# The first weight transfers on ScalarE's queue, and the opening steps of a two-layer encoder in a new order

## The chip, the cores and the metric

The kernel runs on one core of one Trainium2 chip. The metric is the time of one execution on the device in microseconds (us), lower is better; a median of several executions is given. The engines are named as in the profile: PE (TensorE, matrix products), PEld (its weight loads), DVE (VectorE), ACT (ScalarE), POOL (GpSimd) and SP (SyncE, which here only issues transfers). A name with a q (SPq, ACTq) is an engine's instruction queue issuing a transfer.

## The reference, cut to what matters

A sequence of 256 rows of width 1024 passes two layers. Each layer is a half SwiGLU block, a mixer and another half SwiGLU block, each on the normalised rows. The change concerns the first 1.5% of the program: the first SwiGLU block, `swiglu(rmsnorm(x, norm_g[0, 0]), ...)`, and within it the first 512 of 2816 columns.

```python
def rmsnorm(x, g):
    x32 = x.astype(jnp.float32)
    y = x32 * lax.rsqrt(jnp.mean(x32 * x32, axis=-1, keepdims=True) + RMS_EPS)
    return (y * g.astype(jnp.float32)).astype(x.dtype)

def swiglu(h, w_gate, w_up, w_down):
    return (jax.nn.silu(h @ w_gate) * (h @ w_up)) @ w_down

for i in range(DEPTH):
    x = x + MACARON_WEIGHT * swiglu(rmsnorm(x, norm_g[i, 0]), ffn_w_gate[i, 0], ffn_w_up[i, 0], ffn_w_down[i, 0])
    ...
```

## The kernel before, in words

Every float32 product is made of three PE products of rounded halves: a matrix is split into a high part (one ACT copy with rounding, `split_hi`, line 246) and a low part (one subtraction on DVE or POOL, `split_lo`, line 250), and `mm3` (lines 265 to 267) adds high by high, high by low and low by high. The weights pass once: a transfer of 1 MB fills one of two `raw` buffers (four slabs of 128 rows by 512 columns), ACT and DVE split it into one of four `wh` and four `wl` buffers, PE reads these. A `raw` buffer is free for the next transfer when both splits of its four slabs have read it.

The program is a long PE stream; the first chunk of the first block is written out by hand as a list of steps, `START` (line 37), which `first` (line 480) issues one after the other under a manual schedule, so that PE, ACT, DVE and POOL each do their instructions in the order of the list. SP's transfers follow the list too. The steps are:

- `X t.k.n` loads n column blocks of row half t of x; `L u.c.n` loads n slabs of weight unit u from slab c; both on SP. `T` turns x on PE and scales it on DVE, `h` is its high part (ACT), `l` its low part on DVE, `G` its low part on POOL.
- `w u.c` is the high part of a weight slab (ACT), `a u.c` its low part on DVE, `y u.c` its low part on POOL.
- `M m.t.k` is one product of three matmuls: m is gate (0) or up (1), t the row half, k the block of 128 input columns. There are 32, 16 for gate and 16 for up. Block k = 0 must come first in its bank. Units 2 and 3 are the two halves of up, units 0 and 1 of gate; units 4 and 5 belong to the next chunk.
- `D` is a matmul on zeros that keeps PE busy, `g` turns the gains (`norm_g`), `B` and `R` make the row sums and their inverse roots (POOL), `A` applies silu and the product of the two halves.

Behind this list everything else is placed by the framework's scheduler, which estimates times itself and puts each engine's instructions in the order of its estimate; so the order of steps that the diff doesn't name can move as well. In what follows `decay` (line 616) loads a table into a `raw` buffer and takes its absolute value on DVE, `window` (line 621) makes four exponentials of it on ACT, `layer` (line 592) is a small network whose sine is on ACT, and `tr`/`down` (lines 453 and 464) turn the block's result, split it into `ph` and `pl` and multiply it into the `acc` banks. The tables `BUFFERS` (line 80) say which of the rotating buffers each allocation takes.

Of the kernel before, what the change touches and what calls it, by code (L numbers as in the profile page):

```python
# [12 lines left out]
F32 = mybir.dt.float32  # L13
F32R = mybir.dt.float32r
BF16 = mybir.dt.bfloat16
AF = mybir.ActivationFunctionType
# [5 lines left out]
P = 128  # L22
D = 1024
# [6 lines left out]
W = 512  # L30
# [4 lines left out]


START = (
# [7 lines left out]
)  # L45
MIX = (
# [32 lines left out]

BUFFERS = {  # L80
    "mm": (
        "0123012301231023013132103213021302132013201320132012301320132031203120321032103210321021231023102310",
        "2301230123102310321032013201230132013201230123013201321032102310230123102310231232013203103213013210",
        "132302301230132013021322103210320132013210321023102301230132012",
    ),
    "acc": (
        "01230123102301230130213030213021302130213021302012103120312",
# [3 lines left out]
        "010101010101010101010101011010101010101010101010101010101",  # L91
    ),
    "wh": (
        "0123012301230123013021302130213021302130231023102310231023102310231023102310231023102310231023102310",
        "2310231023102310231021302103210321032103210321032103210",
    ),
    "wl": (
        "0123012301230123013021302130213021302130231023102310231023102310231023102310231023102310231023102310",
        "2310231023102310231021032130213021302130213021302130213",
    ),  # L100
    "ph": (
        "012340124301243012432342013240312403124031240314203142031423014201320410214341203412034120341",
# [77 lines left out]
class Net:  # L180
# [139 lines left out]
    def load(self):  # L320
        nc, a, const = self.nc, self.a, self.const
        self.ident = const.tile([P, P], F32, name="ident")
        make_identity(nc, self.ident)
        self.wake = self.scr.tile([P, W], BF16, name="sq", bufs=1)
        nc.vector.memset(self.wake, 0.0)
        self.vr = self.h()[:48, :P]
        nc.sync.dma_start(out=self.vr, in_=a["norm_g"].rearrange("i j (k p) -> (i j k) p", p=P))
        self.x = [const.tile([P, D], F32, name=f"x{t}") for t in range(NT)]
        self.mhalf = const.tile([P, 1], F32, name="mhalf")
        nc.vector.memset(self.mhalf, -0.5)  # L330
        warm = const.tile([P, 1], F32, name="warm")
        nc.scalar.activation(warm, self.mhalf, AF.Silu)
        self.ones = const.tile([P, P], F32, name="ones")
        nc.vector.memset(self.ones, 1.0)
        self.g = const.tile([P, 48], F32, name="g")
        self.gain = lambda i, j: self.g[:, (3 * i + j) * KC:(3 * i + j + 1) * KC]

    def load_gain(self):
        ps = self.bank()
        self.nc.tensor.transpose(out=ps[:, :48], in_=self.vr, identity=self.ident[:48, :48])  # L340
        self.nc.vector.tensor_copy(out=self.g, in_=ps[:, :48])
# [41 lines left out]
    def ffn(self, r, xT, late, wg, wu, wd, finish, hooks=(), early=None, mid=None, pre=None, tail=False):  # L383
        nc, x = self.nc, self.x
# [95 lines left out]
        def first():  # L480

            st, raws, tiles = {}, {}, {}
# [3 lines left out]
                c = slice(k * P, (k + n) * P)  # L486
                nc.sync.dma_start(out=x[t][:, c], in_=self.a["x"][0, halves(t), c])

            def load_w(u, c, n):

                if u not in raws:
                    raws[u] = self.place(self.raw, "raw", U)
                    tiles[u] = self.place(self.wp, "wh", U, F32R), self.place(self.wp, "wl", U, F32R)
                nc.sync.dma_start(out=raws[u].rearrange("p (k c) -> p k c", k=4)[:, c:c + n],
                                  in_=self.rows((wg, wu, wg)[u // 2], u % 2 * 4 + c, n, u // 4 * W, W))

            def turn(t, k, n):
# [8 lines left out]
            def x_parts(t, k, n):  # L506
                return (xh[:, k:k + n, halves(t)], xl[:, k:k + n, halves(t)],
                        st["x", t, k][:, :n * P].rearrange("p (k c) -> p k c", k=n))
# [14 lines left out]
            def rstd(t):  # L523
                r[t], _ = self.rstd([st["s", t, half] for half in range(2)])

            do = {
                "X": load_x, "L": load_w, "D": self.spin, "g": self.load_gain, "T": turn,
                "h": lambda t, k, n: self.split_hi(*x_parts(t, k, n)),
                "l": lambda t, k, n: self.split_lo(*x_parts(t, k, n)),
                "G": lambda t, k, n: self.split_lo(*x_parts(t, k, n), True),  # L530
# [22 lines left out]
        for t in range(NT):  # L553
# [4 lines left out]
            for half in range(2):  # L558
# [3 lines left out]
                n = W // 2 if tail and t and half else W  # L562
# [176 lines left out]
    def mixer(self, hy, mx, cur, nxt, wg, pre, hold, dump=None):  # L739
# [207 lines left out]
        def late_turn():  # L947
            state["late"] = cur["late_turn"]()

        load(6)  # L950
        for c in range(4):
            piece_hi(6, c)
# [42 lines left out]
    def mla(self, ml, cur, nxt, wg, pre, hold, after, dump=None):  # L995
# [314 lines left out]
        def next_split(t, half):  # L1310
            hold[:] = nxt["split"](t, half, state["x", t, half])

        load(0)
        for c in range(4):
            piece_hi(0, c)
# [174 lines left out]
```

## Time and profile before

| | us |
|---|---|
| median of 3 executions | 963.69 |
| lowest, highest | 962.13, 964.54 |
| the profiled execution | 963.41 |
| span in the profile (first to last instruction) | 961.6 |
| PE busy in the span | 950.8 |

The profiled execution spends 1.8 us outside its span. Shares of the span by engine on the chain that ended last, starts and durations of instructions, and the time from issuing a transfer to its landing are used below. A PE row's duration is modelled and overlaps the next row; what a matmul costs is the distance between the starts of two rows, 0.227 us for 512 columns.

### The profile page before, as it was taken

The numbers are of one execution on the slowest core, as the hardware profiler recorded it, in microseconds if no ns is written. First come the engines' busy times: TensorE is split into PE (matmuls) and PEld (weight loads), VectorE is DVE, ScalarE is ACT, GpSimd is POOL, SyncE is SP. The second block draws the span as 40 slices with busy tenths as digits, with TensorE's granted clock in tenths as the row PEclk, the third lists the DMA queues.
The fourth block names the chain that finished last, engine by engine and source line by source line (L and its number), as shares of the span: only waits on it lengthen the run. The fifth ranks groups of instructions, "written<-read, shape, count | busy, mean of one in ns | idle before, by whom it ended". The sixth has DMA issues, their size and how long they took to land.

```text
span 961.6 us, 12376 instructions
## 1 busy us (share of the span) xinstructions
PE 950.8 (99%) x4792; PEld 802.0 (83%) x4792; DVE 592.1 (62%) x786; ACT 495.4 (52%) x780; POOL 179.2 (19%) x228
## 2 busy tenths in 40 slices
PE   9999999999999999999999999999999999999997
PEld 6878888889998888888888888888899888888885
DVE  5577777968876654545565454445787665444454
ACT  5565665447456444445454443334688664333442
POOL 1500441415755100000020000000266510000000
PEclk9999999999999999999999999999999999999999
DMA  7757665436233765455546555554142465556531
GB/s 262 244 178 219 199 235 185 158 100 187 89 132 132 240 215 201 175 175 178 194 139 226 205 182 207 177 210 153 58 135 89 150 222 188 205 178 208 184 132 44
DMA packets 80778, 168.09 MB, mean 175 GB/s; under 512 B 3820, under 2 KB 24181, under 8 KB 80336
## 3 DMA queue, kind: packets, MB, share of 16 engines
q1 hardware_dynamic: 79232, 164.79, 50.3%
q0 software_dynamic: 1200, 1.99, 0.7%
q8 instruction: 37, 0.61, 0.3%
q10 hardware_dynamic: 288, 0.52, 0.1%
q14 instruction: 21, 0.17, 0.1%
HBM read 165.72 MB, written 1.05 MB: 173 GB/s over the span
## 4 chain that ended last, share of the span: by engine, by line
PE 95%; DVE 2%; DMA 1%; issue 1%; ACT 1%; SPq 0%; POOLq 0%; POOL 0%; DVEq 0%; ACTq 0%
PE mm L266 18%; PE mm L265 18%; PE mm L267 18%; PE acc L265 10%; PE acc L267 10%; PE acc L266 10%; PE mm L270 4%; PE acc L789 2%; PE acc L790 1%; PE acc L788 1%; DMA raw<-ffn_w_up 1%; DVE wl L250 0%; PE mm L1272 0%; PE mm L1271 0%; PE mm L1273 0%
## 5 line engine op out<-in xcount | busy, mean ns | idle before, releaser
L250 DVE TENSOR_TENSOR wl<-raw,wh 128x1024 fp32r<-128x1024 f32 (+2 forms) x321 | 350.3, 1122 | 252.8 <-ACT wh L246 252.7
L246 ACT ACTIVATE wh<-raw 128x1024 fp32r<-128x1024 f32 (+3 forms) x370 | 319.7, 904 | 274.0 <-PE mm L267 110.3
L265 PE MATMUL mm<-wh,xTh 128*128 128x512 f32 x704 | 277.1, 394 | 0.2
L267 PE MATMUL mm<-wh,xTl 128*128 128x512 f32 x704 | 274.6, 390 | 0.0
L266 PE MATMUL mm<-wl,xTh 128*128 128x512 f32 x704 | 274.3, 390 | 0.2 <-DVE wl L250 0.2
L266 PEld LDWEIGHTS mm<-wl,xTh 128*128 128x128 f32 x704 | 132.4, 188 | 27.7 <-DVE wl L250 0.5
L267 PEld LDWEIGHTS mm<-wh,xTl 128*128 128x128 f32 x704 | 132.2, 188 | 27.9
L265 PEld LDWEIGHTS mm<-wh,xTh 128*128 128x128 f32 x704 | 132.3, 188 | 27.7 <-ACT wh L246 0.5
L265 PE MATMUL acc<-wh,ph 128*128 128x512 f32 x352 | 139.7, 397 | 0.0
L266 PE MATMUL acc<-wl,ph 128*128 128x512 f32 x352 | 137.8, 392 | 0.0
L267 PE MATMUL acc<-wh,pl 128*128 128x512 f32 x352 | 137.7, 391 | 0.0
L273 POOL TENSOR_TENSOR r<-ms,mhalf 128x1 f32<-128x1 f32 x14 | 16.3, 1165 | 575.8 <-DVE ms L295 575.8
L267 PEld LDWEIGHTS acc<-wh,pl 128*128 128x128 f32 x352 | 66.1, 188 | 13.9 <-DVE pl L250 0.2
L265 PEld LDWEIGHTS acc<-wh,ph 128*128 128x128 f32 x352 | 66.1, 188 | 13.0 <-issue 0.4
L266 PEld LDWEIGHTS acc<-wl,ph 128*128 128x128 f32 x352 | 66.2, 188 | 12.7
L250 POOL TENSOR_TENSOR wl<-raw,wh 128x512 fp32r<-128x512 f32 (+3 forms) x49 | 65.9, 1356 | 28.7 <-ACT wh L246 28.6
L422 ACT ACTIVATE s<-mm,r 128x512 f32<-128x512 f32 (+1 forms) x48 | 31.3, 651 | 65.8 <-PE mm L267 59.2
L250 DVE TENSOR_TENSOR pl<-mm,ph 128x512 fp32r<-128x512 f32 (+1 forms) x66 | 42.9, 653 | 15.2 <-ACT ph L246 15.0
L424 DVE SCALAR_TENSOR_TENSOR h<-mm,r,s 128x512 f32<-128x512 f32 (+1 forms) x48 | 33.8, 703 | 26.9 <-PE mm L267 21.2
L246 ACT ACTIVATE ph<-mm 128x512 fp32r<-128x512 f32 (+1 forms) x66 | 37.0, 562 | 22.5 <-PE mm L270 22.3
L788 PE MATMUL acc<-xTh,wh 128*128 128x256 f32 x128 | 36.9, 288 | 0.0
L270 PE MATMUL mm<-ident,h 128*128 128x128 f32 x240 | 36.5, 272 | 0.0
(316 smaller groups left out, 1089.7 us busy)
## 6 DMA issues: line engine op xcount, KB each, us to landing
raw<-ffn_w_down SPq DMA_DIRECT2D x44, 1024.0 KB, 4.8
raw<-ffn_w_up SPq DMA_DIRECT2D x39, 1024.0 KB, 5.0
raw<-ffn_w_gate SPq DMA_DIRECT2D x38, 1024.0 KB, 5.0
raw<-mix_w_in SPq DMA_DIRECT2D x8, 1024.0 KB, 5.4
raw<-ffn_w_gate SPq DMA_DIRECT2D x8, 512.0 KB, 3.8
raw<-ffn_w_up SPq DMA_DIRECT2D x8, 512.0 KB, 5.0
raw<-mix_w_out SPq DMA_DIRECT2D x4, 1024.0 KB, 4.7
raw<-mla_w_o SPq DMA_DIRECT2D x4, 1024.0 KB, 4.8
```

The lines of the kernel that those rows point to most:

```text
L246: return self.nc.scalar.activation(hi, src, AF.Copy)
L250: return eng.tensor_tensor(out=lo, in0=src, in1=hi.bitcast(F32), op=ALU.subtract)
L265: t.matmul(out=out, lhsT=xh, rhs=wh, start=start, stop=False)
L266: t.matmul(out=out, lhsT=xh, rhs=wl, start=False, stop=False)
L267: t.matmul(out=out, lhsT=xl, rhs=wh, start=False, stop=stop)
L270: self.nc.tensor.transpose(out=out, in_=in_, identity=self.ident)
L273: self.r_ins = self.nc.gpsimd.tensor_tensor(out=out, in0=in_, in1=self.mhalf[:, :1].to_broadcast(list(in_.shape)), op=ALU.pow)
L422: nc.scalar.activation(s[:, :w], ps_g, AF.Silu, scale=r[t])
L424: nc.vector.scalar_tensor_tensor(out=hh[:, :w], in0=ps_u, scalar=r[t], in1=s[:, :w], op0=ALU.mult, op1=ALU.mult)
L788: nc.tensor.matmul(out=ps, lhsT=wh[:, k], rhs=xh[:, k], start=st, stop=False)
L789: nc.tensor.matmul(out=ps, lhsT=wh[:, k], rhs=xl[:, k], start=False, stop=False)
L790: nc.tensor.matmul(out=ps, lhsT=wl[:, k], rhs=xh[:, k], start=False, stop=sp)
```

## The change

Two slabs of the first weight unit (slab 3 and slab 0 of unit 2) are loaded through a new step `Q`, which is `load_w` issued on ScalarE's queue. The load of the gains becomes a step (`N`), and the one small silu that makes ACT load its table becomes a step (`W`) in the middle of the list. The rest of `START` is a new order of the same kinds of steps, with six low parts on POOL (`y2.3`, `y0.0`, `y0.3`, `y1.2`, and `G0.2.2`, `G1.4.4`) where there were two (`G1.0.4`, `y0.0`). Of the tables, `mm`, `wh` and `wl` get new numbers throughout.

```diff
 START = (
-    "D1 X0.0.2 D1 D1 D1 D1 X1.0.4 L2.0.1 L2.3.1 X0.2.2 D1 g X1.4.4 T0.0.2 T1.0.4 L2.1.1 w2.0 L2.2.1 h0.0.2 w2.3 a2.0 "
+    "Q2.3.1 N w2.3 D1 D1 D1 D1 g X1.0.4 Q2.0.1 D1 D1 D1 w2.0 X0.0.2 D1 D1 T1.0.4 X0.2.2 a2.0 D1 L2.1.1 h1.0.4 D1 "
 ...
@@ load
-        self.vr = self.h()[:48, :P]
-        nc.sync.dma_start(out=self.vr, in_=a["norm_g"].rearrange("i j (k p) -> (i j k) p", p=P))
...
-        warm = const.tile([P, 1], F32, name="warm")
-        nc.scalar.activation(warm, self.mhalf, AF.Silu)
+        self.warm = const.tile([P, 1], F32, name="warm")
...
+    def load_norms(self):
+        self.vr = self.h()[:48, :P]
+        self.nc.sync.dma_start(out=self.vr, in_=self.a["norm_g"].rearrange("i j (k p) -> (i j k) p", p=P))
@@ first
-            def load_w(u, c, n):
+            def load_w(u, c, n, queue=nc.sync):
...
-                nc.sync.dma_start(out=raws[u].rearrange("p (k c) -> p k c", k=4)[:, c:c + n],
+                queue.dma_start(out=raws[u].rearrange("p (k c) -> p k c", k=4)[:, c:c + n],
...
-                "X": load_x, "L": load_w, "D": self.spin, "g": self.load_gain, "T": turn,
+                "X": load_x, "L": load_w, "Q": lambda u, c, n: load_w(u, c, n, nc.scalar), "D": self.spin,
+                "N": self.load_norms, "W": lambda: nc.scalar.activation(self.warm, self.mhalf, AF.Silu), "g": self.load_gain, "T": turn,
```

ACT at the start of the program, before: `wh<-raw` is a step w, `xTh<-s` a step h, `sq` a step B.

```order
L332 ACT_TABLE_LOAD
L332 ACTIVATE warm<-mhalf 128x1
L246 ACTIVATE wh_139<-raw_138 128x512
L246 ACTIVATE xTh<-s_153 128x2x128
L246 ACTIVATE wh_139<-raw_138 128x512
L246 ACTIVATE xTh<-s_160 128x4x128
L288 ACTIVATE sq,ss_183<-x_92 128x512
```

The same place after:

```order
L496 DMA raw_123<-ffn_w_up 128x512
L247 ACT_TABLE_LOAD
L247 ACTIVATE wh_124<-raw_123 128x512
L496 DMA raw_123<-ffn_w_up 128x512
L247 ACTIVATE wh_124<-raw_123 128x512
L247 ACTIVATE xTh<-s_158 128x4x128
L289 ACTIVATE sq,ss_170<-x_90 128x512
L247 ACTIVATE wh_124<-raw_123 128x512
```

The second transfer stands behind the first copy (step w2.3), which waits for the first transfer; the copy behind it, w2.0, waits for the second, and so stand the first high part of x and the row sum behind that.

DVE where the first block's low parts `pl` of the turned result are made, before: `raw<-raw` is the absolute value of the decay table, `h` a product with silu.

```order
L250 TENSOR_TENSOR wl_572<-raw_569,wh_571 128x1024 x2
L424 SCALAR_TENSOR_TENSOR h_520<-mm_493,r,s_518 128x512
L250 TENSOR_TENSOR wl_580<-raw_577,wh_579 128x1024 x2
L250 TENSOR_TENSOR pl_541<-mm_535,ph_540 128x512
L619 SCALAR_TENSOR_TENSOR raw_637<-raw_637 128x2048
L424 SCALAR_TENSOR_TENSOR h_558<-mm_522,r,s_556 128x512
L250 TENSOR_TENSOR pl_566<-mm_560,ph_565 128x512
```

The same place after:

```order
L251 TENSOR_TENSOR wl_572<-raw_569,wh_571 128x1024 x2
L251 TENSOR_TENSOR wl_580<-raw_577,wh_579 128x1024 x2
L426 SCALAR_TENSOR_TENSOR h_520<-mm_493,r,s_518 128x512
L622 SCALAR_TENSOR_TENSOR raw_637<-raw_637 128x2048
L251 TENSOR_TENSOR pl_541<-mm_535,ph_540 128x512
L426 SCALAR_TENSOR_TENSOR h_558<-mm_522,r,s_556 128x512
```

The decay table's absolute value has moved ahead of `pl_541`, so that this low part now waits for the decay table's transfer.

ACT a little later, before: `xTl<-raw,negt` and `xTh<-raw,negt` are the four exponentials, `fh` is the sine of the small network.

```order
L246 ACTIVATE ph_540<-mm_535 128x512
L246 ACTIVATE ph_565<-mm_560 128x512
L626 ACT_TABLE_LOAD
L626 ACTIVATE xTl<-raw_637,negt 128x1024
L626 ACTIVATE xTh<-raw_637,negt 128x1024 x2
L626 ACTIVATE xTl<-raw_637,negt 128x1024
L246 ACTIVATE wh_666<-raw_664 128x1024 x2
L612 ACT_TABLE_LOAD
L612 ACTIVATE fh<-arg 64x256
L246 ACTIVATE wh_674<-raw_672 128x1024 x2
```

The same place after:

```order
L629 ACT_TABLE_LOAD
L629 ACTIVATE xTl<-raw_637,negt 128x1024
L629 ACTIVATE xTh<-raw_637,negt 128x1024 x2
L629 ACTIVATE xTl<-raw_637,negt 128x1024
L247 ACTIVATE ph_565<-mm_560 128x512
L247 ACTIVATE wh_666<-raw_664 128x1024 x2
L247 ACTIVATE wh_674<-raw_672 128x1024 x2
L247 ACTIVATE wh_732<-raw_730 128x1024
L615 ACT_TABLE_LOAD
L615 ACTIVATE fh<-arg 64x256
```

The four exponentials now stand ahead of `ph_565`, and the sine stands behind three copies more, the last of which waits for the transfer `raw_730`. The PE product that reads the sine (`mm_625`) stands seven matmuls further back in PE's stream than before.

## Rows read from the trace of the kernel before

**Rows 1.** The page's head, and its shares of the chain that ended last.

```profile
span 961.6 us, 12376 instructions
...
PE 95%; DVE 2%; DMA 1%; issue 1%; ACT 1%; SPq 0%; POOLq 0%; POOL 0%; DVEq 0%; ACTq 0%
```

**Rows 2.** Timeline of PE, 0 to 25 us: start, duration, instruction [idle before].

```profile
7.76 0.99 PE L265 MATMUL mm<-wh,xTh 128*128 128x512 f32 x1
...
9.40 0.47 PE L265 MATMUL mm<-wh,xTh 128*128 128x512 f32 x1
...
22.72 0.39 PE L267 MATMUL mm<-wh,xTl 128*128 128x512 f32 x1
...
24.30 0.40 PE L267 MATMUL mm<-wh,xTl 128*128 128x512 f32 x1
```

**Rows 3.** Timeline of SP's issues, 0 to 80 us (x2: two issues in a row).

```profile
2.12 0.91 SPq L494 DMA_DIRECT2D raw<-ffn_w_up  x2
...
15.86 0.38 SPq L494 DMA_DIRECT2D raw<-ffn_w_up  x1
...
31.74 3.21 SPq L223 DMA_DIRECT2D raw<-ffn_w_up  x2
40.65 3.27 SPq L223 DMA_DIRECT2D raw<-ffn_w_down  x2
50.18 0.34 SPq L618 DMA_DIRECT2D raw<-hyena_decay  x1
...
65.29 7.05 SPq L223 DMA_DIRECT2D raw<-ffn_w_up  x2
```

**Rows 4.** Transfers issued about 1.65, 3.54, 15.86, 40.65, 65.29, 950: size, us to landing.

```profile
x<-x SPq DMA_DIRECT2D x1, 256.0 KB, 3.3
...
x<-x SPq DMA_DIRECT2D x1, 256.0 KB, 5.1
...
raw<-ffn_w_up SPq DMA_DIRECT2D x1, 1024.0 KB, 6.7
...
raw<-ffn_w_down SPq DMA_DIRECT2D x1, 1024.0 KB, 6.0
...
raw<-ffn_w_up SPq DMA_DIRECT2D x1, 1024.0 KB, 5.0
...
out<-s ACTq DMA_DIRECT2D x2, 256.0 KB, 2.5
```

**Rows 5.** Timelines of ACT, DVE and POOL, 0 to 15 us.

```profile
0.73 1.28 ACT L332 ACT_TABLE_LOAD   x1 [0.73 <-PEq L1481]
...
12.96 0.61 ACT L246 ACTIVATE wh<-raw 128x512 fp32r<-128x512 f32 x1
...
13.80 0.68 DVE L250 TENSOR_TENSOR wl<-raw,wh 128x512 fp32r<-128x512 f32 x1
...
11.34 1.39 POOL L250 TENSOR_TENSOR wl<-raw,wh 128x512 fp32r<-128x512 f32 x1 [2.34 <-ACT wh L246]
```

**Rows 6.** Timeline of POOL, 25 to 28 us.

```profile
25.91 1.09 POOL L273 TENSOR_TENSOR r<-ms,mhalf 128x1 f32<-128x1 f32 x1 [13.19 <-DVE ms L295]
...
27.97 0.73 POOL L585 DMA_DIRECT2D zT<-c_zT  x1
```

**Rows 7.** Timelines of DVE, ACT and PE, 53 to 70 us.

```profile
55.00 2.29 DVE L619 SCALAR_TENSOR_TENSOR raw<-raw 128x2048 f32<-128x2048 f32 x1 [1.32 <-DMA raw<-hyena_decay]
...
57.33 1.15 ACT L626 ACTIVATE xTl<-raw,negt 128x1024 f32<-128x1024 f32 x1 [0.49 <-DVE raw L619]
...
61.50 1.99 ACT L246 ACTIVATE wh<-raw 128x1024 fp32r<-128x1024 f32 x2
...
66.41 0.42 ACT L612 ACTIVATE fh<-arg 64x256 f32<-64x256 f32 x1 [1.62 <-DVE arg L609]
...
55.21 0.40 PE L267 MATMUL acc<-wh,pl 128*128 128x512 f32 x1
...
68.26 0.64 PE L599 MATMUL mm<-fh,fw 64*64 64x256 f32 x2
```

More of the change, by code (lines that the diff above doesn't have):

```diff
@@ L81 @@
     "mm": (
-        "0123012301231023013132103213021302132013201320132012301320132031203120321032103210321021231023102310",
-        "2301230123102310321032013201230132013201230123013201321032102310230123102310231232013203103213013210",
-        "132302301230132013021322103210320132013210321023102301230132012",
+        "0123012301230231020221032102310231021302130213021301230213021320132013210321032103210310120312031203",
+        "1230123012031203210321302130123021302130123012302130210321031203123012031203120121302132032102302103",
+        "021231230123021302310211032103213021302103210312031230123021301",
     ),
@@ L93 @@
     "wh": (
-        "0123012301230123013021302130213021302130231023102310231023102310231023102310231023102310231023102310",
-        "2310231023102310231021302103210321032103210321032103210",
+        "0123013201320132012031203120312031203120321032103210321032103210321032103210321032103210321032103210",
+        "3210321032103210321031203102310231023102310231023102310",
     ),
     "wl": (
-        "0123012301230123013021302130213021302130231023102310231023102310231023102310231023102310231023102310",
-        "2310231023102310231021032130213021302130213021302130213",
+        "0123013201320132012031203120312031203120321032103210321032103210321032103210321032103210321032103210",
+        "3210321032103210321031023120312031203120312031203120312",
     ),
```

14 rows, old and new, of the table START are left out of this document.

## The prediction

> **What bounds the kernel now.** I first read the shares of the chain that ended last: PE 95% of a span of 961.6 us [rows 1]. So the end moves by what PE's stream loses or gains in waits, and the change, which leaves the matmuls alone, can act only where PE waits. The timeline of PE's start came next: its first product starts at 7.76, its second at 9.40, and from there matmuls follow each other with hardly a hole until 22.72; there three matmuls that should take 3 x 0.227 = 0.68 us take until 24.30, a stall of 0.90 us in front of the first product that reads unit 3 [rows 2]. That is all the opening has to give: the time before PE runs steadily, and 0.90 us. Then SP's issues, because buffers of `raw` are handed on from transfer to transfer up to about 70 us [rows 3], and last what ACT, DVE and PE do between 53 and 70 us, where the order moved as well [rows 7].
>
> **Part 1, the first transfers on ACT's queue.** ACT's first instruction stands at 0.73 [rows 5]; I put the issue of slab 3 there. The table load of 1.28 us, which now stands behind it, ends before the slab lands and costs nothing. A 256 KB transfer took 3.3 us when issued early in a burst and 2.5 us alone, at the end of the program [rows 4]. I take 3.0: slab 3 lands at 3.75. The second transfer, slab 0, stands in ACT's order behind the copy w2.3. That copy waits for slab 3, so on ACT's queue slab 0 is issued no earlier than 3.75, where SP issued its slab 0 at 2.12 [rows 3]. By 3.75 SP has sent about five transfers, one per 0.45 us or so; behind roughly 1 MB, a 256 KB transfer issued at 3.54 took 5.1 us [rows 4]. Bounds for slab 0: 2.5 us (as if alone) to 5.1 + 0.65 (at the end of SP's backlog, with one more transfer of that size at the 1 MB in 5 us or so of rows 4 ahead), so landing between 6.25 and 9.5. I take 4.0, the middle, as if the two queues share: landing at 7.75.
>
> The Trainium skill, "DMA: Bandwidth & Descriptors", section "Issuing engines are not separate DMA queues", speaks against this part: transfers started by any engine run on the same 16 DMA engines and interleave, and a second issuer saves only sequencer time. By it the gain of part 1 would be at most SP's issue time ahead of slab 0, not a landing of its own; that lies within the bounds above, and no run here has shown it yet.
>
> Behind slab 0: copy w2.0 0.61 [rows 5], done at 8.4; its low part on DVE 0.68, done at 9.1; the low part of x, l1.0.4, the same size, at 9.75 with hand-overs. It is the third matmul of the first product that reads it, so that product ends at about 9.98. In the kernel before, when the second product starts at 9.40, one product and four turns (about 0.35 us of PE at full rate) were done [rows 2]; afterwards the turns lie ahead of it, or are to come, 0.58 + 0.35 = about 0.9 us later. The steps that follow (w2.1, w2.2, the other turns and low parts) have their inputs by then, if their SP transfers keep their pace. **PE runs 0.9 us late at 10 us**; from -0.8 (landing 6.25) to +2.6 (landing 9.5).
>
> **Part 2, the stall before unit 3.** The first product on unit 3 is now the 22nd of the 32, not the 21st, 0.68 us further back, and unit 3's transfer is issued about where it was, 15.86 [rows 3], and takes 6.7 us [rows 4]. With PE 0.9 us late and one product more ahead, the transfer lands in time: -0.90. Moving the table load (W) into the list puts 1.28 us [rows 5] and a small activation between two copies of unit 3; cover is the copies' lead over PE, part of which is gone: 0.3, between 0 and 0.5. The six low parts on POOL at 1.39 instead of 0.68 us on DVE [rows 5] lie beside products; POOL stands idle for long, 13.19 us of waiting for DVE alone in one place [rows 6]. Nothing, as long as PE reaches each of them 1.4 us after its copy. **Opening in all: 0.9 - 0.9 + 0.3 = +0.3 us**, from -1.4 (landing 6.25) to +2.0 (landing 9.5).
>
> **Part 3, what moved behind the list.** The low parts of unit 4 (a4.x) no longer stand behind A0, the silu and product; the `raw` buffer comes free sooner and the pair of issues at 31.74 [rows 3] comes about 1.9 us earlier. Each later transfer into `raw` waits for the splits of the one two before it, so the chain of issues 31.74, 40.65, 50.18 [rows 3] moves with it: the decay table, in use on DVE at 55.00 [rows 7], lands at D = 53.0 instead of 54.9 (bounds 51.4, if unit 3 lands a further 1.7 us sooner, and 54.9, if nothing is handed on).
>
> Against that stand two new waits. (a) `pl_541` now waits behind the absolute value: D + 0.1 + 2.29 + 0.7 = D + 3.1, while PE wants it at 55.21 [rows 7]; with D = 53.0 that is 56.1, 0.9 us late. Queued behind it are PE's `acc` products, and nobody else. (b) The sine. From D: absolute value done 2.4; four exponentials 57.33 to 61.50, 4.2; `ph_565` 0.6; the copies of raw_664 1.99 [rows 7]; its last low part about 1.2 (twice 0.68, less a fixed part), which frees the buffer for raw_730; landing 5.0 [rows 4]; first half of its copy 1.0; table load 1.28; sine 0.42; hand-overs 0.2: D + 18.3. PE used the sine at 68.26 [rows 7], and now seven matmuls later, 68.26 + 1.6 = 69.85. With D = 53.0 it is there at 71.3, +1.45; with D = 51.4 in time; with D = 54.9, +3.4. These waits don't add to the opening's lag: whatever PE is already late shortens them, so the end moves by the largest of them. Opening +0.3, (a) +0.9, (b) between 0 and +1.45 with D between 51.4 and 53.0: I take **+1.0 us**, the value for D = 52.55.
>
> **The rivals.** *A, slower: slab 0 at the end of SP's backlog.* Its place is ACT's queue: if the 16 DMA engines serve SP's earlier packets first, the slab lands at 9.5 rather than 7.75, the opening ends 2.0 late, and since units 3 and 4 start later too, D comes to about 54.5 and the sine at 72.8, +3.0 or a little more: 963.41 + 3.3 = 966.7. It decides once slab 0 lands later than 8.9 or D is later than 54.3. For it: the 5.1 us of the transfer issued at 3.54 [rows 4]; against it: that transfer stood in SP's own queue, slab 0 stands in another.
>
> *B, better: the second transfer doesn't wait for the copy.* If ACT's sequencer sends slab 0 while w2.3 still waits, it leaves at about 1.2 and lands by 5.6; the first product's third matmul starts near 8.2, 1.55 before my 9.75, so the opening comes out 1.25 us ahead (0.3 - 1.55), D near 51.4, and (a) and (b) take about 0.4 of that back: 963.41 - 0.8 = 962.6, between 961.9 and 963.3. For it stands nothing in the rows; against it stands POOL, where the issue of zT, free of any wait of its own, left only at 27.97, behind an instruction that had waited 13.19 us and ran at 25.91 [rows 6]. POOL is another engine, though. The Trainium skill, "Perfetto Trace Analysis", section "DVE / Act Engine Instruction (TENSOR_ADD, Activation, etc)", has an instruction wait for its semaphore in a queue of its own while the sequencer goes on, which is the rule behind B; the trace shows it nowhere, and for POOL it shows the opposite.
>
> *C, nothing changes:* opening and later waits within 0.3 us of before, because the transfers in sum limit the opening either way; 963.4. It falls inside the forecast's range.
>
> **How the numbers follow.** The profiled execution took 963.41, the median 963.69, so they stand 0.3 us apart and I set the sum on the former. Forecast: 963.41 + 1.0 = 964.4, with a range of its own from 962.9 (D = 51.4, slab 0 early) to 966.2. Chances: forecast .56, A .17, B .22, C and others .05. The range takes in nearly all of B and A but its far end: 961.5 to 967.2. 0.3%, about what a measurement of this kernel can tell from no change, is 2.9 us: faster means below 960.8, slower above 966.6. Only the far end of B (landing 6.25 or sooner, D in time) and what I can't name reach the first: .06. Slower are most of A (.15) and the upper end of the forecast (.03): .18. The same: .76.
>
> **What would show it.** In the profile after, step by step: slab 0's issue on ACTq near 3.8 (at 1.2: B is right); its landing near 7.75 (9.5: A); PE's third matmul of the first product near 9.75; no stall in front of the first product of unit 3; the issue on SP at 31.74 found near 30; the decay table's absolute value starting near 53 on DVE; a PE wait of about 1 us ahead of the third `acc` matmul on `pl`, and another ahead of the matmul on `fh`, released by ACT. I am wrong if PE's waits up to 70 us sum to less than before without B, which would mean that the opening had more slack than its timeline shows; if unit 3's transfer is late all the same; or if a wait of PE of some us shows a lowered granted clock behind it, which I have not priced.

## The result: slower by 7.3 us, and the profile after

The changed kernel takes 970.64 us (median of 6, 969.98 to 971.60) against 963.39 us (median of 6): a ratio of 1.0076, 95% interval 1.0066 to 1.0085. The prediction said 964.4, with 967.2 as its upper end. The profiled execution took 969.98 us.

The page's head and its chain, of the kernel after:

```profile
span 968.2 us, 12376 instructions
...
PE 89%; DMA 4%; DVE 3%; ACT 2%; issue 1%; POOLq 0%; POOL 0%; DVEq 0%; ACTq 0%; SPq 0%
```

The span is 6.6 us longer than in [rows 1], and PE's share of the chain has fallen from 95% to 89%: transfers, DVE and ACT now stand on the path. Some of its longest pieces, of the kernel after (start, us, what), show which:

```profile
3.73 5.24 DMA raw<-ffn_w_up
10.19 0.80 PE mm L266
...
19.79 4.96 DMA raw<-ffn_w_up
...
46.32 6.00 DMA raw<-ffn_w_down
...
55.78 0.74 DVE h L426
56.52 2.21 DVE raw L622
```

**The second slab.** ACT's timeline after, 0 to 14 us (start, duration, instruction, idle before and what ended it), and PE's:

```profile
0.74 0.41 ACTq L496 DMA_DIRECT2D raw<-ffn_w_up  x1
...
3.72 0.63 ACT L247 ACTIVATE wh<-raw 128x512 fp32r<-128x512 f32 x1 [1.25 <-DMA raw<-ffn_w_up]
3.73 0.34 ACTq L496 DMA_DIRECT2D raw<-ffn_w_up  x1
8.99 0.63 ACT L247 ACTIVATE wh<-raw 128x512 fp32r<-128x512 f32 x1 [4.64 <-DMA raw<-ffn_w_up]
9.53 0.61 ACT L247 ACTIVATE xTh<-s 128x512 fp32r<-128x512 f32 x1
```

```profile
10.19 0.80 PE L266 MATMUL mm<-wh,xTh 128*128 128x512 f32 x1 [3.20 <-ACT xTh L247]
10.79 0.63 PE L267 MATMUL mm<-wl,xTh 128*128 128x512 f32 x1
```

Slab 0 is issued at 3.73, the moment the copy in front of it starts, and its own copy starts at 8.99. PE's first product waits 3.20 us, not for the slab itself but for the high part of x (`xTh`), which stands behind that copy on ACT. The kernel before started its first product at 7.76 [rows 2].

**What PE's clock did.** Busy time by stretch, after (us, their sum, PE, PEld, DVE, ACT, POOL busy, granted clock, DMA share, GB/s):

```profile
6.00:9.40 3.40, 0.99 (x7) 0.56 (x5) 0.69 (x1) 0.41 (x1) 0.00 (x0) 1.00 1.01 374
9.40:12.00 2.60, 1.81 (x4) 1.38 (x5) 2.20 (x5) 2.56 (x8) 0.00 (x0) 0.50 0.81 307
12.00:16.20 4.20, 4.20 (x11) 3.27 (x10) 2.70 (x3) 2.66 (x6) 3.75 (x3) 0.50 0.00 1
16.20:20.00 3.80, 3.80 (x22) 3.15 (x22) 2.16 (x4) 1.44 (x4) 0.79 (x2) 1.00 0.83 271
```

Behind the wait, from 9.4 to 16.2 us, the granted clock is 0.50, the lower of the two levels (1.2 GHz), and matmuls start 0.43 us apart instead of 0.227.

**The later waits.** DVE and PE of the kernel after, from 50 to 75 us; the rows of before are in [rows 7]:

```profile
53.50 2.36 DVE L251 TENSOR_TENSOR wl<-raw,wh 128x1024 fp32r<-128x1024 f32 x2 [3.45 <-ACT wh L247]
55.78 0.74 DVE L426 SCALAR_TENSOR_TENSOR h<-mm,r,s 128x512 f32<-128x512 f32 x1
56.44 2.28 DVE L622 SCALAR_TENSOR_TENSOR raw<-raw 128x2048 f32<-128x2048 f32 x1
58.64 0.68 DVE L251 TENSOR_TENSOR pl<-mm,ph 128x512 fp32r<-128x512 f32 x1
```

```profile
59.38 0.50 PE L268 MATMUL acc<-wh,pl 128*128 128x512 f32 x1 [0.22 <-DVE pl L251]
...
75.00 0.64 PE L602 MATMUL mm<-fh,fw 64*64 64x256 f32 x2 [0.82 <-ACT fh L615]
```

The DVE rows begin with the splits of raw_577, a weight transfer of `ffn_w_down` whose high part ACT starts here after, and here before:

```profile
52.41 2.01 ACT L247 ACTIVATE wh<-raw 128x1024 fp32r<-128x1024 f32 x2 [3.22 <-DMA raw<-ffn_w_down]
```

```profile
49.23 2.01 ACT L246 ACTIVATE wh<-raw 128x1024 fp32r<-128x1024 f32 x2 [0.53 <-DMA raw<-ffn_w_down]
```

How late PE is against the kernel before, worked out as the difference between the starts of PE's matmul of the same number, counted from 0, in the two traces (both have 4792), with the experiments that are told below:

| PE matmul (start before, us) | after | e1 | e10 | e13 |
|---|---|---|---|---|
| no. 60 (16.82) | +4.73 | +1.06 | +0.56 | +0.30 |
| no. 200 (49.52) | +3.77 | +0.10 | +0.94 | -0.66 |
| no. 250 (60.00) | +4.26 | +1.74 | +0.94 | -0.66 |
| no. 320 (76.46) | +5.17 | +2.51 | +1.66 | +0.06 |
| no. 3300 (668.49) | +4.87 | +2.63 | +2.01 | +0.20 |
| no. 4500 (890.63) | +6.60 | +3.47 | +1.05 | -0.02 |

The opening loses 3.8 us, the waits for `pl` and the sine 0.5 and 0.9, and 1.7 us more go at 695 to 715 us, where each engine's rows stand in the same order before and after (the last section takes that place up). Executions of one program differ by 2 us and more (962.13 to 964.54 before, 969.98 to 971.60 after), so a column is one example; what a part costs is read from the medians below.

### The profile page after: what moved, and what is told of

It reads as the page before. It is cut to its first block, busy times and chain, and to the rows that moved or that the text cites. A ratio compares the mean times of both kernels' runs of the same rounds, so it can differ in the third digit from the quotient of the medians.

```text
span 968.2 us, 12376 instructions
## 1 busy us (share of the span) xinstructions
PE 953.1 (98%) x4792; PEld 803.5 (83%) x4792; DVE 592.4 (61%) x782; ACT 497.0 (51%) x781; POOL 182.7 (19%) x232
## 3 DMA queue, kind: packets, MB, share of 16 engines
q10 hardware_dynamic: 576, 1.05, 0.3%
HBM read 165.72 MB, written 1.05 MB: 172 GB/s over the span
## 4 chain that ended last, share of the span: by engine, by line
PE 89%; DMA 4%; DVE 3%; ACT 2%; issue 1%; POOLq 0%; POOL 0%; DVEq 0%; ACTq 0%; SPq 0%
PE mm L268 17%; PE mm L266 17%; PE mm L267 16%; PE acc L266 9%; PE acc L268 9%; PE acc L267 9%; PE mm L271 4%; DMA raw<-ffn_w_up 2%; PE acc L792 2%; PE acc L793 1%; PE acc L791 1%; DVE wl L251 1%; ACT wh L247 1%; DMA raw<-ffn_w_down 1%; DMA raw<-ffn_w_gate 1%
## 5 line engine op out<-in xcount | busy, mean ns | idle before, releaser
L251 DVE TENSOR_TENSOR wl<-raw,wh 128x1024 fp32r<-128x1024 f32 (+3 forms) x318 | 347.7, 1124 | 255.8 <-ACT wh L247 255.5
L251 POOL TENSOR_TENSOR wl<-raw,wh 128x512 fp32r<-128x512 f32 (+3 forms) x52 | 70.8, 1372 | 29.2 <-ACT wh L247 29.0
```

What stands on the lines that cost most here:

```text
L251: return eng.tensor_tensor(out=lo, in0=src, in1=hi.bitcast(F32), op=ALU.subtract)
```

## The experiments

Each kernel was timed beside the kernel before on the same chip, and ratios are to that.

**e1: slab 0 issued ahead of the copy.**

```diff
-    "Q2.3.1 N w2.3 D1 D1 D1 D1 g X1.0.4 Q2.0.1 D1 ...
+    "Q2.3.1 Q2.0.1 N w2.3 D1 D1 D1 D1 g X1.0.4 D1 ...
```

> The changed kernel, with the issue of slab 0 moved ahead of the copy w2.3 on ACT's queue (directly behind slab 3's issue) and nothing else. Theory W (the loss is the wait: slab 0 stands behind a copy that waits, lands at 8.9, PE idles 3.2 us, and the lowered clock that follows costs about 2.8 more): slab 0 is issued near 1.2 and lands by 5.5, PE's first product starts by 7.7 instead of 10.19, products stand 0.227 apart from there, and the time falls by 4 to 5.5 us to 965 to 966.5, not further, since the sine is then up to 1.5 us more late. Rival N (the rest of the new order is at fault, such as low parts on POOL): 969.5 or more, with the first product early all the same. Rival Q (whatever stands on ACT's queue is served behind SP's transfers, however early it is issued): slab 0 lands after 7, the time stays above 968.5.

Measured: ratio 1.0039 (1.0025 to 1.0052), 968.16 us against 964.60. PE's first product starts at 8.08, the granted clock is 1.00 from 9.2 us on, and at 50 us PE is 0.10 late instead of 3.77. So about half of the loss was the place of the second slab's issue, as theory W had it. The other half stayed: 3.6 us above the kernel before by the medians, where I expected 1.6 to 3.1. Its place, in e1, DVE's and then PE's timeline:

```profile
50.97 2.36 DVE L251 TENSOR_TENSOR wl<-raw,wh 128x1024 fp32r<-128x1024 f32 x2 [3.91 <-ACT wh L247]
53.24 0.74 DVE L426 SCALAR_TENSOR_TENSOR h<-mm,r,s 128x512 f32<-128x512 f32 x1
53.91 2.28 DVE L622 SCALAR_TENSOR_TENSOR raw<-raw 128x2048 f32<-128x2048 f32 x1
56.10 0.68 DVE L251 TENSOR_TENSOR pl<-mm,ph 128x512 fp32r<-128x512 f32 x1
```

```profile
55.07 0.40 PE L267 MATMUL acc<-wl,ph 128*128 128x512 f32 x1
56.84 0.50 PE L268 MATMUL acc<-wh,pl 128*128 128x512 f32 x1 [1.38 <-DVE pl L251]
```

The four DVE rows follow each other without a hole: the low part `pl` is behind the splits of raw_577, a product and the absolute value, and PE waits 1.38 us for it.

**e2: PE kept busy through the wait.**

```diff
-    ... h1.0.4 D1 l1.0.4 B1.0 T0.0.2 w2.1 h0.0.2 T0.2.2 L2.2.1 ...
+    ... h1.0.4 l1.0.4 B1.0 T0.0.2 w2.1 h0.0.2 T0.2.2 D13 L2.2.1 ...
```

> The changed kernel with 13 matmuls on zeros in place of one, between the last turn and the first product on PE (12 more matmuls in all, in a bank that the first product takes next), so that PE is busy through the wait for slab 0. The wait itself stays. Theory W: the granted clock stays at 1.00 from 6 us on, the first 27 matmuls stand 0.227 apart instead of 0.427, and the time falls by 2.5 to 3 us, to 967.6 to 968.1; the first product still starts near 10.2. Rival: the pace of 0.427 has another cause (weight loads, reads next to transfers): it stays, and the time is 970.6 or up to 0.5 above.

(In the changed list two steps D stand between Q2.0.1 and w2.0, not three as in the diff ahead of the prediction.)

Measured: ratio 1.0080 (1.0062 to 1.0099): no gain where 2.5 to 3 us were expected; by the two intervals a gain of more than about 1.6 us is excluded (an estimate). The clock part held: the granted clock is 1.00 from 7.0 us on, and matmuls of the first products start 0.23 us apart. The time didn't follow. PE of e2:

```profile
7.55 2.97 PE L349 MATMUL mm<-sq 128*128 128x512 bf16 x13
11.12 0.51 PE L266 MATMUL mm<-wh,xTh 128*128 128x512 f32 x1 [0.60 <-ACT xTh L247]
...
30.43 0.50 PE L267 MATMUL mm<-wl,xTh 128*128 128x512 f32 x1 [0.43 <-DVE wl L251]
```

In this execution slab 0 was later still (first product at 11.12). The thirteenth matmul of the products starts at 14.33 against 15.48 after: from a start 0.93 us later the clock gave 2.1 us by there. The nineteenth stands at 17.05 against 17.56, the 61st at 27.18 against 27.68 and the 71st at 30.43 against 29.94: 0.64 us is waited away for the weights that come next, the rest and more in front of unit 3. So in part the lower clock fills time in which PE would have waited; how much of the rest is the late slab of this one execution stays open, but no gain shows in the median. Whether the slab was later by chance or by the edit is open too.

**e3: both slabs back on SP, in the same places of the list.**

```diff
-    "Q2.3.1 N w2.3 D1 D1 D1 D1 g X1.0.4 Q2.0.1 ...
+    "L2.3.1 N w2.3 D1 D1 D1 D1 g X1.0.4 L2.0.1 ...
```

> The changed kernel with both first transfers (slab 3, slab 0) issued on SP at the same places in the list, and nothing else: only the queue is undone. Theory W: slab 0 leaves SP near 2.1, behind slab 3, the gains and one transfer of x, and lands near 5.5; PE's first product starts before 8 and the clock stays up; 965 to 966.5, within 0.8 us of the kernel with slab 0's issue ahead of the copy. Rival N: 969.5 or more.

Measured: ratio 1.0040 (1.0024 to 1.0055), the same as e1. No cost of the queue alone shows if nothing stands in front of the issue. The medians lie 3.1 us apart, the ratio stands for 3.9, at or above the upper end of the 1.6 to 3.1 expected.

**e4: the kernel before, with only the queue changed.**

```diff
-    "D1 X0.0.2 D1 D1 D1 D1 X1.0.4 L2.0.1 L2.3.1 X0.2.2 ...
+    "Q2.0.1 Q2.3.1 W D1 X0.0.2 D1 D1 D1 D1 X1.0.4 X0.2.2 ...
```

> The kernel before with slab 0 and slab 3 issued as the first two instructions on ACT's queue, ahead of the table load and of every copy, and SP's other transfers unchanged: the queue alone. Theory W says nothing against it: slab 0 lands near 3.5 instead of 5.64, the first product can start up to 1 us earlier, but the transfers behind it carry the same bytes, so that PE waits later for part of it: 962.9, between 962.2 and 963.6. By the page on transfers of the Trainium skill (DMA: Bandwidth & Descriptors, a second issuer saves only the issue time): 963.0 to 963.5. A gain of over 1.2 us would mean that the opening of the kernel before is bounded by the first slab alone.

Measured: ratio 1.0002 (0.9990 to 1.0014). It neither gains nor loses. The first product didn't come sooner, since PE now waited for the blocks of x:

```profile
4.69 0.66 PE L270 MATMUL mm<-ident,x 128*128 128x128 f32 x2 [0.49 <-DMA x<-x]
5.68 1.09 PE L270 MATMUL mm<-ident,x 128*128 128x128 f32 x4 [0.33 <-DMA x<-x]
...
8.34 0.99 PE L265 MATMUL mm<-wh,xTh 128*128 128x512 f32 x1
```

That no gain shows agrees with the rule that the prediction cites from the Trainium skill, "DMA: Bandwidth & Descriptors", section "Issuing engines are not separate DMA queues".

**e5: the kernel before, with the first product on unit 3 one product later.**

```diff
-    ... w3.0 M1.0.5 w4.3 a3.0 M0.1.2 M0.1.7 ...
+    ... w3.0 M0.1.2 w4.3 a3.0 M1.0.5 M0.1.7 ...
```

> The kernel before with the first product on unit 3 (M1.0.5) put one product later (M0.1.2 ahead of it), nothing else: what the stall of 0.90 us ahead of unit 3 is worth by itself. If PE's time is what bounds the opening: the stall shrinks by 0.68, PE is that much earlier at 25 us, and the time falls by 0.5 to 0.9 us (ratio 0.9992 to 0.9995). Rival (the opening is bounded by the chain of transfers through the two raw buffers): PE is earlier at 25 us, but a wait behind it takes the gain back, and the time stays within 0.2 us.

Measured: ratio 0.9999 (0.9990 to 1.0007). PE went from 0.24 late at matmul 80 to 0.14 late at matmul 100, a gain of 0.10 where 0.68 was expected. By one execution it can't be told whether unit 3 was only later by chance; in the median no gain is seen.

**e6: e1 with the sine ahead of the copies of raw_730.**

```diff
 ...
+                if late:
+                    with self.tc.issue_after(self.sine):
+                        self.split_hi(wh[:rows, c:e], wl[:rows, c:e], raw[:rows, c:e])
 ...
```

> The kernel of e1_slab0_first (slab 0 issued ahead of the copy) with both copies of raw_730 queued on ACT behind the first sine of the small network; PE's matmul on fh comes one product sooner by that. By the step on the sine: the wait of PE at 71 us ahead of that matmul, 0.8 to 1.0 us, is gone, PE is 0.7 to 1.0 earlier at 100 us, and the time lies 0.7 to 1.0 us below that of e1_slab0_first (ratio about 1.003). Rival: the copies of raw_730, now 0.6 us later, make the products that read them wait, and less than 0.3 us is left.

Measured: ratio 1.0038 (1.0026 to 1.0049). The wait for the sine is gone from the trace (PE is as late at matmul 320 as at 250, 3.06 us), but the time is that of e1. Under 1 us can't be told from the spread of executions here; the wait was real, its worth by itself stays open.

**e8: e6 with the absolute value behind `pl` on DVE.**

```diff
 ...
-            nc.vector.scalar_tensor_tensor(out=raw, in0=raw, scalar=-1.0, in1=raw, op0=ALU.mult, op1=ALU.max)
+            with self.tc.issue_after(self.first_low):
+                nc.vector.scalar_tensor_tensor(out=raw, in0=raw, scalar=-1.0, in1=raw, op0=ALU.mult, op1=ALU.max)
```

> The kernel of e6_sine_first, in which also the decay table's absolute value is queued on DVE behind the first pl; the scheduler then orders some rows between 50 and 100 us anew. By the step on pl: PE's wait of 1.5 us ahead of the third acc matmul at 55 us is gone, and the time lies 2 to 2.5 us below e1_slab0_first, 1 to 1.5 above the kernel before (ratio 1.001 to 1.002). Rival: with the absolute value and the exponentials later, the transfer behind the decay table comes later, and a wait for it between 60 and 75 us takes back more than half.

Measured: ratio 1.0073 (1.0061 to 1.0085), worse than e6. The wait for `pl` is gone (PE is 0.30 late at matmuls 200 and 250), but the scheduler then put the copies of raw_664 ahead of the exponentials on ACT, and the rest behind them:

```profile
63.57 0.47 PE L273 MATMUL mm<-wh,xTh 128*128 128x512 f32 x1 [2.19 <-DVE v L385]
...
66.29 0.80 PE L273 MATMUL acc<-wh,ph 128*128 128x512 f32 x1 [0.54 <-ACT ph L254]
```

The granted clock is 0.50 from 63.9 to 70.7 us, and PE is 6.2 us late at matmul 320. One edge is not an experiment on one wait where a scheduler orders the rest.

**e10: e6 with that `pl` made on POOL, every other row nearly in place.** ACT copies the bank plainly behind `ph_540`, POOL subtracts, and the exponentials are ordered behind that copy on ACT.

```diff
 ...
+                self.plain = self.scr.tile([P, 512], F32, name="s0", bufs=1)[:, :w]
 ...
+                self.plain_ins = self.nc.scalar.activation(self.plain, ps[:, :w], AF.Copy).ins
+                self.split_lo(hi[:, :w], lo[:, :w], self.plain, True)
 ...
```

> The kernel of e6_sine_first, with the first pl (pl_541) made on POOL out of a plain copy of the bank that ACT makes behind ph_540 (one ACT copy more, one DVE subtraction less); the absolute value and the exponentials keep their places. In the runs so far pl_541 was done 7.0 us after raw_577 landed (49.79 and 56.78 in e1_slab0_first; 52.32 and 59.32 in the changed kernel; 51.12 and 58.12 in e6_sine_first), because DVE has the splits of raw_577, a product and the absolute value ahead of it. If that chain of DVE is what PE waits for at 55 us, the wait of 1.2 to 3.6 us ahead of the third acc matmul is gone, PE at 60 us is as late as at 50 us, and the time lies 1 to 2 us below e6_sine_first (ratio 1.001 to 1.003). Rival: the transfers of raw_577 and raw_664 themselves hold PE up by then, and a wait for them between 58 and 70 us takes it back.

Measured: ratio 1.0009 (1.0000 to 1.0019). POOL's and PE's rows of e10:

```profile
53.85 1.29 POOL L258 TENSOR_TENSOR pl<-s,ph 128x512 fp32r<-128x512 f32 x1 [10.00 <-ACT s L474]
```

```profile
55.93 0.39 PE L274 MATMUL acc<-wl,ph 128*128 128x512 f32 x1
56.16 0.40 PE L275 MATMUL acc<-wh,pl 128*128 128x512 f32 x1
```

`pl` is done at 55.14 and PE passes without a wait; 0.7 us of smaller waits remain between 60 and 72 us. With slab 0, the sine and `pl` mended, the changed opening costs about what the old one did. Theory W, widened by what DVE and ACT do ahead of `pl` and the sine, goes with nearly all of the loss; the edit also takes away a delay of 0.7 us near 695 us (last section), so not all of it is the two waits.

**e11: e10 with slab 0's issue behind the copy again.**

```diff
-    "Q2.3.1 Q2.0.1 N w2.3 D1 D1 D1 D1 g X1.0.4 D1 ...
+    "Q2.3.1 N w2.3 D1 D1 D1 D1 g X1.0.4 Q2.0.1 D1 ...
```

> The kernel of e10_pl_on_pool, with slab 0's issue back behind the copy w2.3, as in the changed kernel: the late slab by itself, with the later waits for pl and the sine taken away. If PE is late at the end by the largest of the lags and not by their sum, this kernel loses what the opening loses, 3.8 us at 50 us, and hardly more at 100 us, so that it lies only 1 to 1.5 us below the changed kernel (ratio 1.006 to 1.0065), and about 3 us above e10_pl_on_pool. If the lags add, it lies 2.5 us or more below the changed kernel.

Measured: ratio 1.0041 (1.0028 to 1.0054). The late slab costs 0.0032 against e10, about 3.1 us, as expected. But e11 lies 0.0035, 3.4 us, below the changed kernel, where I expected 1 to 1.5. The four corners:

| ratio to before | later waits as changed | later waits mended |
|---|---|---|
| slab 0 behind the copy | 1.0076 (after) | 1.0041 (e11) |
| slab 0 ahead of it | 1.0039 (e1) | 1.0009 (e10) |

By the medians the two causes add: 0.0032 to 0.0037 for the slab and 0.0030 to 0.0035 for the later waits, whichever is mended first. What is left over for the sum, 0.0005, is known to about 0.0023 (an estimate from the four intervals), so that the one covering up to 1.7 us of the other isn't excluded; that all the later waits are covered is. Nor are the later waits gone in e11's profiled execution, at 972.03 us 3.7 above its median:

```profile
59.97 0.50 PE L275 MATMUL acc<-wh,pl 128*128 128x512 f32 x1 [1.17 <-POOL pl L258]
...
66.89 0.50 PE L273 MATMUL acc<-wh,ph 128*128 128x512 f32 x1 [0.96 <-ACT ph L254]
```

There the copies of raw_577 started only at 55.34, and the plain copy that POOL reads stood behind them on ACT. So the column "mended" holds for e10 and in part for e11.

**e12: the other transfers put behind slab 0.**

```diff
-    ... X1.0.4 Q2.0.1 ... L2.1.1 h1.0.4 ... L2.2.1 L0.3.1 ... L0.0.1 w2.2 X1.4.4 L0.1.1 a2.2 X0.4.4 ... L0.2.1
+    ... X1.0.4 Q2.0.1 Q2.1.1 Q2.2.1 Q0.3.1 Q0.0.1 ... h1.0.4 Z1.4.4 Q0.1.1 Z0.4.4 Q0.2.1 ...
```

(`Z` is a transfer of x issued on ACT; eight transfers have moved from SP to ACT, not nine as written beforehand.)

> The changed kernel, in which slab 0 is still issued behind the copy w2.3 on ACT, but nine transfers of the opening that SP issued up to there or soon after (five slabs and more of units 2 and 0, two of x) are issued on ACT behind it; SP keeps the gains, the three first blocks of x and unit 1. It asks what holds slab 0 from 3.73 to 8.9 us. If it is the order of issue (the DMA engines serve what SP issued before it first): with 0.75 MB in all issued ahead instead of about 1.3 MB, slab 0 lands by 6.6, PE's first product starts near 8.2, and the time falls by 2 to 4 us (ratio 1.003 to 1.0055; ACT spends up to 3.5 us on issuing, which can delay copies). If ACT's queue is slow by itself, slab 0 lands after 8 as before and the time is 970 or more (1.007 or above).

Measured: ratio 1.0035 (1.0023 to 1.0048). ACT of e12, then PE:

```profile
3.81 1.31 ACTq L496 DMA_DIRECT2D raw<-ffn_w_up  x3
...
7.50 0.63 ACT L247 ACTIVATE wh<-raw 128x512 fp32r<-128x512 f32 x1 [3.07 <-DMA raw<-ffn_w_up]
```

```profile
8.70 0.50 PE L266 MATMUL mm<-wh,xTh 128*128 128x512 f32 x1 [1.75 <-ACT xTh L247]
```

Issued at the same time, still behind the copy, slab 0's copy starts at 7.50 instead of 8.99 (6.6 was expected): what held it, for 1.5 us at least, was what SP had issued ahead, and ACT's queue isn't slow by itself. (The granted clock was 0.50 here too, from 9.4 to 12.8 us.) The traffic of the kernel after shows the same thing; by queue (packets, MB, share of the 16 engines; q1 is SP's, q10 ACT's), first of 3.75 to 6.25 us, then of 6.25 to 8.9 us:

```profile
q1 hardware_dynamic: 484, 0.65, 82.1%
```

```profile
q1 hardware_dynamic: 412, 0.75, 75.8%
q10 hardware_dynamic: 144, 0.26, 26.0%
```

For 2.5 us after its issue not one packet of slab 0 moved; then all 0.26 MB did, side by side with SP's (from 7 to 8 us 125 packets of ACT's queue and 93 of SP's).

**e9: e6 with four small memsets on DVE at its start.** This asks for the 0.7 us near 695 us.

```diff
-    "Q2.3.1 Q2.0.1 N w2.3 ...
+    "Q2.3.1 Q2.0.1 N P4 w2.3 ...
```

> The kernel of e6_sine_first with four memsets of one column each on DVE at its start, where it is idle until 3 us; every other row on every engine stands in the same order, and DVE has 788 rows as in the kernel before, against 784 in the changed one. It asks for the 0.7 us that every kernel with the changed opening loses near 695 us, 630 us behind the last row whose order differs: there DVE's tensor_tensor h<-kr takes 1.03 us instead of 0.29, behind a split on POOL that starts just ahead of it, because the row before it on DVE starts 0.15 us late. If that delay comes from where the rows lie in DVE's instruction stream, the wait of 0.7 us is gone here, and the time is 0.5 to 0.8 below e6_sine_first. If it comes from the data's timing, the wait stays, and the time is within 0.3 us of e6_sine_first.

Measured: ratio 1.0055 (1.0035 to 1.0075). The wait near 695 us stayed, so the number of rows ahead on DVE isn't its cause. In its profiled execution PE was on time at 50 us (+0.02) and 5.0 us late at 60: it waited 3.17 us for `pl`, and the granted clock was 0.50 from 59.4 to 62.8 us. The copies of raw_577 started at 51.36 there, 2.1 us later than before, and `pl` stood behind them: in this execution an opening on time was worth nothing.

**e13: e10 with W at the start of ACT.**

```diff
-    "Q2.3.1 Q2.0.1 N w2.3 ... W a1.3 ...
+    "Q2.3.1 Q2.0.1 W N w2.3 ... a1.3 ...
```

> The kernel of e10_pl_on_pool with the small silu W as the third instruction on ACT, behind the two transfers, instead of between the first and the second copy of unit 3; one table load less. In the profile of e10_pl_on_pool PE waits 0.46 and 0.70 us ahead of the products of unit 3 at 26 to 27 us, for a copy and a split that stand behind that table load of 1.28 and the silu of 0.20. By the step on W: that wait is gone when unit 3 lands about 22.8, PE at 30 us is 0.7 to 1.1 earlier, and the time is 0.3 to 1.1 us below e10_pl_on_pool: ratio to the kernel before 0.9997 to 1.0006. Rival: the wait for unit 3 is one for its transfer, and the first copy waits as long: no change (1.0005 to 1.0013).

Measured: ratio 1.0016 (1.0005 to 1.0028). In e10, ACT and PE around unit 3:

```profile
23.45 1.28 ACT L544 ACT_TABLE_LOAD   x1
```

```profile
26.04 0.49 PE L273 MATMUL mm<-wh,xTh 128*128 128x512 f32 x1 [0.30 <-ACT wh L254]
26.97 0.50 PE L274 MATMUL mm<-wl,xTh 128*128 128x512 f32 x1 [0.44 <-DVE wl L258]
```

In e13 those waits are gone and PE is 0.66 us ahead of the kernel before from 27 to 60 us, the best opening of all. In the median nothing of it is left, against the 0.3 to 1.1 us expected: the intervals of e10 and e13 overlap, and neither beats the kernel before. The profiled execution of e13 (963.58) is the fastest of its twelve, 2.4 us below their median.

## Why the prediction was wrong

The sum gave +1.0 us, and 7.3 were measured, beyond the upper end of 967.2 too. Two steps failed. Part 1 sized the landing of slab 0 too small and priced no lowered clock: it had PE 0.9 us late at 10 us and 0.3 late behind unit 3; PE was 4.7 late at 17 us and 3.8 at 50. Part 3 let the later waits disappear in that lag; by the four corners they cost about 0.0030 to 0.0035 on top of it. (The lower bounds of parts 1 and 2 are also 0.2 off: 1.5 us less than 0.9 and 0.3 is -0.6 and -1.2. Nothing came near them.)

**Slab 0's landing (part 1): mechanism right, size off.** The issue at 3.73 was as forecast. I took 4.0 us to the landing, the middle between alone and behind SP's backlog; it was 5.1 to 5.2, so the copy started at 8.99, not 7.75. Of the two bounds, the row of the transfer issued at 3.54 [rows 4] was the right one to take: e12 and the packets by queue show that what SP had issued first went first. The section of the Trainium skill that the prediction cites here ("DMA: Bandwidth & Descriptors", "Issuing engines are not separate DMA queues") is borne out in that a second issuer brought no gain of its own (e4, 1.0002). That the transfers interleave shows here only late: the second queue got nothing for 2.5 us, and from 7 to 8 us the two moved packets side by side. Rival A had this place, at a chance of .17, but its price of 3.3 us was less than half of what came.

**The first product (part 1): a step missing.** I let the first product start early and put only its third matmul behind slab 0. Its first matmul reads `xTh`, whose copy I had listed as standing behind w2.0 on ACT, and forgot there. The product that I had ending at 9.98 started at 10.19, and PE waited 3.20 us for it. By itself the step costs little: the third matmul, forecast for 9.75, started at 11.21, and 1.24 of that is the landing.

**The clock: not priced.** I named a lowered clock as what could make me wrong, and it came behind PE's wait, from 9.4 to 16.2 us. In the kernel after, the first product starts 2.11 us later than in e1, and at matmul 60 PE is 3.67 later than there: 1.56 went in that stretch. In e2, with the clock up, 3.04 at the first product are 3.17 at matmul 60. But e2's median didn't gain by it: with the clock kept up, PE waits for weights instead, and the ratio stays at 1.0080. So the clock explains 1.6 of the 4.7 us at 17 us in one execution, and no part of the median is shown to be its own. (1.06 of the 4.7 stands in e1 too, where slab 0 is in time.)

**The stall before unit 3 (part 2): right, and worth little.** PE of after gains 0.96 us between matmuls 80 and 100, where 0.90 was forecast. But it gains it because it is late. In e5 the kernel before gained 0.10 of 0.68 at that place, and nothing in the median. W I priced at 0.3; in e10, where PE is 0.6 us late, it costs 1.16 (two distances of 0.69 and 0.93 us instead of 0.227), and in the changed kernel and e1, where PE is later, nothing.

**The wait for `pl` (part 3a): right place, wrong chain.** I had `pl` done at D + 3.1, by the landing of the decay table. In e1 the decay chain did come sooner, as forecast (its issue at 47.08 instead of 50.18), yet the absolute value started at 53.91. It stood behind the splits of raw_577, which use the other `raw` buffer. From the start of raw_577's copy to the end of `pl` it takes 6.9 us: 52.41 to 59.32 after, 49.87 to 56.78 in e1. I followed one of the two chains of buffers and the DVE rows of the other stood in front of it, as the order that I had quoted showed (`wl_580`, `h_520`, then the absolute value).

**"These waits don't add": wrong.** I let the end move by the largest lag. The four corners show a sum, within some 2 us. When slab 0 is late, unit 2's splits are late, its `raw` buffer comes free late, and so every transfer behind it: unit 3 is issued at 19.79 instead of 15.86 [rows 3], and raw_577's copy starts at 52.41 instead of 49.23. DVE and ACT move with PE for the most part, so PE's lag covers little of what they are late. It covers some: in the kernel after, PE at 50 us is 3.7 us later than in e1 and raw_577's copy only 2.5, and PE's lag grows by 0.5 at `pl` instead of 1.6. But 0.5 and 0.9 came on top of the opening's 3.8, where the prediction's rule leaves nothing.

**The sine (part 3b): right.** From the start of the absolute value to PE's matmul on the sine I had 18.2 us; it took 18.6 after (56.44 to 75.00) and 18.5 in e1. PE's lag grew by 0.9 there after and by 0.8 in e1. e6 takes that away from the trace; the time doesn't show it.

**Rival B fell.** The issue left at 3.73, 0.01 us behind the start of the copy that it stood behind. The rule of the Trainium skill ("Perfetto Trace Analysis", section "DVE / Act Engine Instruction (TENSOR_ADD, Activation, etc)") that a sequencer goes on while an instruction waits isn't borne out by this trace for a transfer on ACT behind a copy: the issue left 0.01 us behind the copy's start, not 2.5 us ahead of it; POOL's rows [rows 6] told it rightly.

## What to carry to other kernels

A transfer moved to a compute engine's queue stands in that engine's order: put its issue ahead of everything that waits, or it leaves later than it would on SP, and with a backlog in front of it. When buffers hand transfers on in a chain, a lag at its head moves the other engines along; expect later waits to come on top of it and at most in part to vanish in it. For a low part on DVE, count every row in front of it, those of the other buffer too, and ask what PE wants first.

## What the hardware showed beyond that

- **Order of issue across queues.** A 256 KB transfer on ACT's queue, issued when SP had some 1.3 MB ahead, moved its first packets more than 2.5 us later (3.75 to 6.25 us: none of 484). How far this goes by the order of issue in general, no run asks.
- **A third queue in front of raw_577.** In e1 that transfer is issued at 43.89, and from 43 to 46 us POOL's queue, with small tables of the mixer, moved 0.52 MB and SP's 0.11. Before, POOL's 0.53 MB passed from 40 to 43 us, ahead of it. From its issue to the start of its copy raw_577 took 5.7 us before, 6.0 in e1 and 4.9 to 7.7 in all the profiled executions. How much of the wait for `pl` is this scatter, no run isolates.
- **A race far behind the change.** Near 695 us seven kernels (after, e1, e2, e3, e6, e9, e12) have one DVE row of 1.0 us that takes 0.29 in the others (before, e4, e5, e8, e10, e11, e13), next to a split on POOL. DVE, then POOL of the kernel after, and the same of the kernel before:

```profile
696.30 1.03 DVE L1070 TENSOR_TENSOR h<-kr 128x128 f32<-128x128 f32 x1
```

```profile
696.17 1.01 POOL L251 TENSOR_TENSOR wl<-raw,wh 128x384 fp32r<-128x384 f32 x1
```

```profile
691.28 0.29 DVE L1067 TENSOR_TENSOR h<-kr 128x128 f32<-128x128 f32 x1
```

```profile
691.29 1.15 POOL L250 TENSOR_TENSOR wl<-raw,wh 128x384 fp32r<-128x384 f32 x1
```

  The DVE row that starts 0.01 us ahead of POOL's takes 0.29; the one that starts 0.13 behind it takes 1.03 and ends 0.15 behind POOL's end. PE waits 0.55 us for it. What puts the row before it 0.15 us later stays open: with four more DVE rows ahead, in e9, it stayed. It is a part, some 0.7 us, of what e10 mends beside the two waits.
- **The clock at the same place.** Behind PE's wait of 2.1 us for the next such row, the granted clock of the kernel before is 0.50 (1.2 GHz) from 694.7 to 698.1 us; after, behind a wait of 1.95 us, it is so from 702.3 to 705.7, and 1.0 of the 1.7 us that go at 695 to 715 go around that stretch. In e5, e8, e10 and e13 the clock stays at 1.00 there, and PE makes good about 1.0 us (e10: from 2.02 late to 1.05). e5 is the kernel before but for the place of one product, so this isn't what was mended; whether it goes by program or by execution, one profile each can't tell. It flatters the last rows of the columns e10 and e13.
- **Where the rest lies.** e10 is still 0.0009 above the kernel before, at the edge of its interval; no experiment names a cause for that.
